# Finer weight pieces at the start of a hybrid decoder, and a final norm whose mean is summed on TensorE

## The chip, the cores and the metric

The kernel runs on one core of a Trainium2 chip. The metric is the device time of one launch in microseconds (us), lower is better. The engines of the core are TensorE (PE in the profile, with PEld for its weight loads), VectorE (DVE), ScalarE (ACT), GpSimd (POOL) and SyncE (SP, which here only issues transfers). Each engine takes its instructions from its own queue, and semaphores order them between engines.

## What is computed

One inference step of a decoder with two layers. Layer 0 mixes tokens with a short gated convolution, layer 1 with retention; behind each comes a SwiGLU feed-forward network, and at the end an RMS norm:

```python
def rmsnorm(x, g):
    y = x * rsqrt(mean(x * x, axis=-1) + 1e-6)
    return y * g

def short_conv_mixer(x, buf, w_in, w_conv, w_out):
    b, c, h = split(x @ w_in, 3)              # w_in: 1024 x 3072
    u = c * h
    full = concatenate([buf, u])
    y = sum(w_conv[j] * full[:, j:j+L] for j in range(3))
    return (b * y) @ w_out, full[:, -2:]

for i in range(2):
    x = x + mixer[i](rmsnorm(x, norm_mix[i]))  # short conv, then retention
    x = x + swiglu(rmsnorm(x, norm_ffn[i]))
y = rmsnorm(x, final_norm)
```

There are 512 prompt tokens and 8 x 4 sample tokens, 544 in all, with a model width of 1024 in fp32. The new convolution and retention states are outputs too.

## The kernel before

**Layout.** The activations stand transposed: x[kt], kt = 0 to 7, is a tile of 128 partitions (128 of the 1024 features) by 544 columns (the tokens). The columns are worked in two halves of 272 (HT): a matmul writes one half, `half(pt, hf)`. To keep fp32 accuracy with TensorE's faster type, every operand is split into a high and a low part, and each product is three matmuls: high weight by high activation, high weight by low activation, low weight by high activation (`project`, L187). A weight piece is loaded into a tile w; ScalarE copies the high part out of it (wh, L202) and VectorE subtracts to get the low part (wl, L203); `split` is the helper. The same is done for x by `split_x` (L221 on ScalarE, L222 on VectorE), which also multiplies in the norm's gain. The norm's own factor is taken out of the products: since it is one number for each token, the products start with x unscaled, and the factor is multiplied in later.

**The norm's factor.** `square_sum` squares a tile on ScalarE and adds it up on VectorE in sqacc. In the first stage and in several others it uses one buffer for the squares, sqlast (L238, added at L239; the last tile's at L234, L235). `rms_scale` then forms the mean over the features with matmuls that have sqacc as the stationary operand (L271, cb being the column of 1/1024), adds eps on VectorE (L244), takes the power −1/2 on GpSimd (L247, rN), and spreads the result over all partitions by a matmul against the identity (L251). The result is the row R.

**The start.** `start()` loads three weight pieces of 1024 columns (cvin 0 to 2, one for each of b, c and h) and the eight x tiles, and runs the products k tile by k tile as they come: for each of the eight k tiles, three pieces by three matmuls by two halves, 18 matmuls. So that k tile 0 can start early, each piece is loaded and split in column parts: first 128 columns (k tile 0), then k tiles 1 to 3 (384 columns), then 4 to 7 (512). The loads go out on SyncE's queue in the program's order, x[1], the second parts, x[2], x[3], the third parts, and so on; the splits are chained in the same order by `issue_after`, one behind the other, and behind the last one come the squares of x.

**The final norm.** `final` works on the last three output tiles (n = 5, 6, 7) of layer 1's feed-forward network, half by half. `products(hf)` makes the three products and adds them to x (L901), and squares each. `scale(hf)` is the norm's factor for one half: three sums of 128 columns or less (L919), eps (L920), pow (L921), then behind a `yield` the spread over the partitions (L251). `gained(hf)` multiplies x by the final gain into ya (x[0] to x[3]) and yb (x[4] to x[7]) at L911. `out(hf, y, w)` multiplies two of the tiles by the factor and stores them: for w = 0 ScalarE copies the factor to R (L932) and GpSimd does the multiplications (L934); for the others VectorE does (L936). The stores (L938) go out on ScalarE's queue for even w, on SyncE's for odd w. `idle(n, ins)` (L947) issues matmuls of ones whose result nobody reads.

**What sets the order.** The kernel is written in a tile framework: the program states what is done, a scheduler orders each engine's instructions, and `issue_after` binds an instruction behind another. Each engine then runs its instructions in the order given. In `final` the generators `products` and `scale` are advanced by hand (`next`, `drain`), which is how half 0's norm comes to stand among half 1's products.

## Time and profile before

| | |
|---|---|
| median of 3 runs | 1410.4 us (1409.67 to 1411.84) |
| the profiled execution | 1408.96 us, span 1407.2 us |
| granted TensorE clock, mean | 0.999 |
| TensorE busy | 1393.3 us (99%) |
| VectorE busy | 1133.3 us (81%) |
| ScalarE busy | 821.1 us (58%) |
| GpSimd busy | 216.2 us (15%) |
| moved by DMA | 233.82 MB, mean 166 GB/s |

How to read it: the span is from the first to the last instruction of the profiled execution, and the time of that execution holds a little more around it. Times in the timeline count from the span's start. A row of the timeline has the start, the length, the engine, the line, the operation, what is written and read, the shapes, and how many alike follow; in brackets stands how long the engine was idle before it and what ended that. The median of the runs and the profiled execution are different executions of the same program.

### The profile page before, as it was taken

How to read it: one execution, taken by the hardware profiler on the slowest of the kernel's cores; microseconds unless marked ns; L12 is line 12 of the kernel's file. 1: busy time of each engine (PE TensorE's matmuls, PEld its weight loads, DVE VectorE, ACT ScalarE, POOL GpSimd, SP SyncE). 2: the span in 40 equal slices, each digit the busy share in tenths (PEclk: the TensorE clock that was granted, in tenths of full speed). 3: DMA queues.
4: the chain of work that ended last, by engine and by line, in shares of the span. 5: the costliest groups of instructions: out<-in, count | busy, mean ns of one | idle time of the engine just before them, and what ended most of it. 6: DMA issues, size and time to landing. Idle time of an engine off the chain costs nothing.

```text
span 1407.2 us, 26615 instructions
## 1 busy us (share of the span) xinstructions
PE 1393.3 (99%) x10478; PEld 1320.4 (94%) x10478; DVE 1133.3 (81%) x1930; ACT 821.1 (58%) x1281; POOL 216.2 (15%) x248
## 2 busy tenths in 40 slices
PE   9999999999999999999999999999999999999997
PEld 8999999999999999999977877877899999999997
DVE  6987889898989878667867686585799898989884
ACT  6666567677667657667531413213387767677654
POOL 0111011222221214111000000010111212121212
PEclk9999999999999999999999999999999999999999
DMA  6466347768686745677567355375766777776742
GB/s 206 122 165 166 108 108 159 171 166 185 141 192 151 171 112 149 183 192 204 173 244 237 122 208 184 119 260 180 210 143 152 168 176 171 155 184 152 166 104 87
DMA packets 99246, 233.82 MB, mean 166 GB/s; under 512 B 9744, under 2 KB 33312, under 8 KB 98736
## 3 DMA queue, kind: packets, MB, share of 16 engines
q1 hardware_dynamic: 67696, 167.04, 38.0%
q0 software_dynamic: 28688, 56.61, 23.4%
q10 hardware_dynamic: 2736, 8.46, 1.6%
q8 instruction: 82, 1.34, 0.4%
q14 instruction: 44, 0.36, 0.1%
HBM read 191.97 MB, written 28.42 MB: 157 GB/s over the span
## 4 chain that ended last, share of the span: by engine, by line
PE 91%; DVE 4%; DMA 2%; ACT 1%; issue 1%; POOL 0%; SPq 0%; DVEq 0%; POOLq 0%; ACTq 0%
PE sm L385 43%; PE mm L385 16%; PE mm L187 13%; PE sm L187 5%; PE sm L1231 2%; PE sm L1229 2%; PE sm L1230 2%; PE sm L175 1%; PE sm L176 1%; PE sm L177 1%; PE sm L1452 1%; PE mm L1237 1%; DMA S<-in_rets_dram 1%; PE mm L1470 0%; DVE ol L203 0%
## 5 line engine op out<-in xcount | busy, mean ns | idle before, releaser
L385 PE MATMUL sm<-oh,wh 128*128 128x272 f32 x856 | 247.8, 289 | 0.5 <-DVE b L446 0.5
L385 PE MATMUL sm<-ol,wh 128*128 128x272 f32 x856 | 246.1, 288 | 0.0
L385 PE MATMUL sm<-oh,wl 128*128 128x272 f32 x856 | 246.1, 287 | 0.0
L202 ACT ACTIVATE h<-w 128x1024 fp32r<-128x1024 f32 (+3 forms) x170 | 136.6, 804 | 106.2 <-PE mm L385 92.9
L203 DVE TENSOR_TENSOR l<-w,h 128x1024 fp32r<-128x1024 f32 (+3 forms) x170 | 153.6, 905 | 28.1 <-ACT h L202 25.1
L314 ACT ACTIVATE wh<-w 128x1024 fp32r<-128x1024 f32 (+1 forms) x134 | 133.7, 998 | 56.9 <-PE sm L385 48.6
L385 PEld LDWEIGHTS sm<-oh,wh 128*128 128x128 f32 x856 | 161.3, 188 | 2.0 <-DVE b L446 0.9
L385 PEld LDWEIGHTS sm<-oh,wl 128*128 128x128 f32 x856 | 161.0, 188 | 0.0
L385 PEld LDWEIGHTS sm<-ol,wh 128*128 128x128 f32 x856 | 160.8, 188 | 0.1
L202 ACT ACTIVATE wh<-w 128x1024 fp32r<-128x1024 f32 (+3 forms) x76 | 67.7, 897 | 149.6 <-PE mm L187 92.9
L385 PE MATMUL sm<-parts,wh 128*128 128x272 f32 x736 | 142.5, 288 | 0.0
L317 POOL DMA_DIRECT2D wl<-in_ffgu_dram x87 | 81.7, 939 | 328.2 <-ACT wl L316 94.3
L385 PE MATMUL mm<-oh,h 128*128 128x272 f32 x396 | 115.5, 292 | 0.0
L385 PEld LDWEIGHTS sm<-parts,wh 128*128 128x128 f32 x736 | 115.5, 188 | 0.0
L385 PE MATMUL mm<-oh,l 128*128 128x272 f32 x396 | 113.5, 287 | 0.0
L385 PE MATMUL mm<-ol,h 128*128 128x272 f32 x396 | 113.3, 286 | 0.0
L315 DVE TENSOR_TENSOR wl<-w,wh 128x512 fp32r<-128x512 f32 (+1 forms) x134 | 87.3, 651 | 26.5 <-ACT wh L314 26.2
L385 PE MATMUL sm<-parts,wl 128*128 128x272 f32 x368 | 106.2, 289 | 0.3 <-DMA wl<-in_rtqk_dram 0.2
L316 ACT ACTIVATE wl<-wh 128x512 fp32r<-128x512 f32 (+1 forms) x173 | 102.9, 595 | 2.0
L203 DVE TENSOR_TENSOR wl<-w,wh 128x1024 fp32r<-128x1024 f32 (+3 forms) x76 | 79.5, 1055 | 12.6 <-ACT wh L202 12.2
L187 PE MATMUL mm<-parts,wh 128*128 128x272 f32 x488 | 83.1, 291 | 1.4 <-ACT wh L202 1.0
L385 PE MATMUL sm<-oh,h 128*128 128x272 f32 x284 | 82.3, 290 | 0.5 <-ACT g L444 0.3
(380 smaller groups left out, 3842.1 us busy)
## 6 DMA issues: line engine op xcount, KB each, us to landing
w<-in_ffgu_dram SPq DMA_DIRECT2D x66, 512.0 KB
wl<-in_ffgu_dram POOLq DMA_DIRECT2D x87, 256.0 KB, 5.2
S<-in_rets_dram SPq DMA_DIRECT2D x16, 1024.0 KB
out_rets_dram<-S SPq DMA_DIRECT2D x16, 1024.0 KB
w<-in_ffdn_dram SPq DMA_DIRECT2D x36, 384.0 KB
cb<-in_ffgu_dram SPq DMA_DIRECT2D x22, 512.0 KB
w<-in_cvin_dram SPq DMA_DIRECT2D x21, 512.0 KB
wl<-in_ffdn_dram POOLq DMA_DIRECT2D x48, 192.0 KB, 4.7
```

Source lines behind the costliest of these rows:

```text
L175: nc.tensor.matmul(out, lh, rh, start=start, stop=False, skip_group_check=True)
L187: last_product[0] = nc.tensor.matmul(half(pt, hf)[:, :HT], w[:, c], act[k][:, hf * HT : (hf + 1) * HT], start=(first and k == ks[0] and i ...
L202: h = nc.scalar.activation(dh, src, AF.Copy)
L203: last_low[0] = nc.vector.tensor_sub(dl, src, dh.bitcast(F32))
L314: nc.scalar.activation(wh, w, AF.Copy)
L315: last_mixed[0] = nc.vector.tensor_sub(wl[:, :n], w[:, :n], wh[:, :n].bitcast(F32))
L316: nc.scalar.activation(wl[:, n:], wh[:, n:].bitcast(F32), AF.Copy, scale=-1.0)
L317: nc.gpsimd.dma_start(wl[:, n:], src[:, 1, :] if len(src.shape) == 3 else src[:, n:], accum_op=ALU.add)
L385: last = nc.tensor.matmul(out, w[:, c], b, start=(first and j == 0 and i == 0), stop=(j == len(self.ks) - 1 and i == 2), skip_group_check= ...
L1229: nc.tensor.matmul(out, xh[kt][:, ts_], wh[:, cw], start=(kt == 0), stop=False)
L1230: nc.tensor.matmul(out, xh[kt][:, ts_], wl[:, cw], start=False, stop=False)
L1231: last = nc.tensor.matmul(out, xl[kt][:, ts_], wh[:, cw], start=False, stop=(kt == KT - 1))
```

## The change

The change has two parts.

In `start()` the three weight pieces come in five column parts, 128, 128, 256, 256 and 256 columns, where there were three of 128, 384 and 512. The second to fifth parts are loaded behind x[1], x[2], x[4] and x[6], where the second and third came behind x[1] and x[3]. Behind the first part there are thus 12 loads for 6, and 12 splits for 6.

In `final` half 1's products are issued in two parts of two and the remaining k tiles, so that other work can stand between them. Half 0's mean moves from behind product n = 5 of half 1 into the middle of n = 6, and half 0's spread from behind n = 7 into the middle of n = 7. In half 1 VectorE no longer adds the last square to sqacc: the means are summed over sqacc and sqlast by two groups of matmuls into the same place. The four idle matmuls go, the five remain. The outputs of half 0 are bound anew: w = 2 behind the last addition to x, half 1's eps behind the output of w = 2, w = 3 behind that eps.

```diff
     def square_sum(kt, pool, tag="sq", ..., add=None, apart=False):
...
             last_square[0] = nc.scalar.activation(sqlast[:, c], x[kt][:, c], AF.Square)
-            nc.vector.tensor_add(sqacc[:, c], sqacc[:, c], sqlast[:, c])
+            if not apart:
+                nc.vector.tensor_add(sqacc[:, c], sqacc[:, c], sqlast[:, c])
...
-            parts = [slice(0, P), slice(P, KP * P), slice(KP * P, KT * P)]
+            parts = [slice(0, P), slice(P, 2 * P), slice(2 * P, 4 * P), slice(4 * P, 6 * P), slice(6 * P, KT * P)]
...
                 nc.sync.dma_start(x[kt], a["xT"][kt])
-                if kt in (1, 3):
+                if kt in (1, 2, 4, 6):
                     for p in pieces:
-                        p[2](parts[1 + kt // 3])
-                        steps.append(lambda p=p, kt=kt: p[3](parts[1 + kt // 3]))
+                        p[2](parts[1 + kt // 2])
+                        steps.append(lambda p=p, kt=kt: p[3](parts[1 + kt // 2]))
...
-                project(pt, wh, wl, 0, ah, al, hfs=(hf,))
-                nc.vector.tensor_add(x[n][:, c], x[n][:, c], half(pt, hf)[:, :HT])
-                square_sum(n, tp, "gu", 4, c=c, add=nc.vector)
+                if hf:
+                    project(pt, wh, wl, 0, ah, al, last=False, hfs=(hf,), ks=range(2))
+                    yield
+                    project(pt, wh, wl, 0, ah, al, first=False, hfs=(hf,), ks=range(2, len(ah)))
+                else:
+                    project(pt, wh, wl, 0, ah, al, hfs=(hf,))
+                last_add[0] = nc.vector.tensor_add(x[n][:, c], x[n][:, c], half(pt, hf)[:, :HT])
+                square_sum(n, tp, "gu", 4, c=c, add=nc.vector, apart=hf == 1)
                 yield
...
-            for i, at in enumerate((0, P, HT - P)):
-                cols = slice(hf * HT + at, hf * HT + at + P)
-                last_sum[hf] = nc.tensor.matmul(mq[:, i : i + 1], sqacc[:, cols], mean_w[:, 0:1], start=True, stop=True)
-            nc.vector.tensor_scalar_add(rN[:, :3], mq, EPS)
+            for t in (sqacc, sqlast)[: hf + 1]:
+                for i, at in enumerate((0, P, HT - P)):
+                    cols = slice(hf * HT + at, hf * HT + at + P)
+                    last_sum[hf] = nc.tensor.matmul(
+                        mq[:, i : i + 1], t[:, cols], mean_w[:, 0:1],
+                        start=(t is sqacc and (i == 0 or not hf)), stop=(t is sqlast or not hf), skip_group_check=True,
+                    )
+            with tc.issue_after(last_out[0].ins) if hf else ExitStack():
+                last_eps[0] = nc.vector.tensor_scalar_add(rN[:, :3], mq, EPS)
...
         first, second = scale(0), products(1)
-        next(second)
+        for _ in range(3):
+            next(second)
         next(first)
         y0 = gained(0)
-        drain(second)
+        for _ in range(2):
+            next(second)
         drain(first)
         out(0, y0, 0)
         out(0, y0, 1)
-        idle(4, last_spread[0].ins)
+        drain(second)
+        with tc.issue_after(last_add[0].ins):
+            out(0, y0, 2)
         rest = scale(1)
         with tc.issue_after(last_spread[0].ins):
             next(rest)
         idle(5, last_sum[1].ins)
         y1 = gained(1)
-        out(0, y0, 2)
-        out(0, y0, 3)
+        with tc.issue_after(last_eps[0].ins):
+            out(0, y0, 3)
```

The scheduler makes of this the following. First ScalarE behind the first stage, where the squares of x and the splits of the next weights stand; x_74 to x_81 are x[0] to x[7], wh_354 and its like the high parts of the next 1024-column weights (other numbers in the changed program), b_111 and c_110 the copies of the first products. Before:

```order
L238 ACTIVATE sqlast<-x_76 128x544
L238 ACTIVATE sqlast<-x_77 128x544
L238 ACTIVATE sqlast<-x_78 128x544
L202 ACTIVATE wh_354<-w_353 128x1024
L238 ACTIVATE sqlast<-x_79 128x544
L593 ACTIVATE b_111<-mm_203 128x544
L593 ACTIVATE c_110<-mm_204 128x544
L202 ACTIVATE wh_418<-w_417 128x1024
L238 ACTIVATE sqlast<-x_80 128x544
```

After:

```order
L239 ACTIVATE sqlast<-x_76 128x544
L239 ACTIVATE sqlast<-x_77 128x544
L202 ACTIVATE wh_372<-w_371 128x1024
L239 ACTIVATE sqlast<-x_78 128x544
L594 ACTIVATE b_111<-mm_221 128x544
L594 ACTIVATE c_110<-mm_222 128x544
L202 ACTIVATE wh_436<-w_435 128x1024
L239 ACTIVATE sqlast<-x_79 128x544
L202 ACTIVATE wh_498<-w_497 128x1024
L239 ACTIVATE sqlast<-x_80 128x544
```

The first weight's split has moved ahead of the square of x[4], and the following squares stand behind more of other work.

Then ScalarE at the end of the program, with the semaphores that each instruction waits for (none are named where an engine waits for nothing new). Before:

```order
L238 ACTIVATE sq_16318<-x_80 128x272 [waits DVE_49,Activation_49]
L911 ACTIVATE yb_16364<-x_78,vec 128x272 [waits Activation_49]
L911 ACTIVATE yb_16364<-x_79,vec 128x272
L234 ACTIVATE sqlast<-x_81 128x272 [waits DVE_49]
L932 ACTIVATE R<-sm_16288 128x272 [waits PE_49]
L911 ACTIVATE yb_16364<-x_80,vec 128x272
L911 ACTIVATE yb_16364<-x_81,vec 128x272
L938 DMA out_yT_dram<-ya_16294 128x544 [waits Pool_49]
L938 DMA out_yT_dram<-yb_16295 128x544 [waits DVE_49,Activation_49]
L932 ACTIVATE R<-sm_16351 128x272 [waits PE_49]
```

After:

```order
L239 ACTIVATE sq_16336<-x_80 128x272 [waits DVE_49,Activation_49]
L943 ACTIVATE R<-sm_16313 128x272 [waits PE_49]
L917 ACTIVATE yb_16381<-x_78,vec 128x272 [waits Activation_49]
L917 ACTIVATE yb_16381<-x_79,vec 128x272
L949 DMA out_yT_dram<-ya_16319 128x544 [waits Pool_49]
L234 ACTIVATE sqlast<-x_81 128x272 [waits DVE_49]
L917 ACTIVATE yb_16381<-x_80,vec 128x272
L949 DMA out_yT_dram<-yb_16320 128x544 [waits DVE_49,Activation_49]
L917 ACTIVATE yb_16381<-x_81,vec 128x272
L943 ACTIVATE R<-sm_16365 128x272 [waits DVE_49,PE_49]
```

Half 0's copy of R and the store of ya, which waits for GpSimd, have moved ahead of the square of x[7].

Last, TensorE at the end of the program; sm_16288 (before) and sm_16313 (after) hold half 0's factor, sm_16351 and sm_16365 half 1's, sm_16321 and sm_16339 the product n = 7 of half 1. Before:

```order
L187 MATMUL sm_16321<-ol_11792,wh_16217 128x272
L187 MATMUL sm_16321<-oh_11791,wl_16218 128x272
L251 MATMUL sm_16288<-cb,rN 128x128 x2
L251 MATMUL sm_16288<-cb,rN 128x16
L947 MATMUL sm_16346<-ones 128x128 x4
L919 MATMUL sm_16351<-cb,sqacc 128x1 x3
L947 MATMUL sm_16357<-ones 128x128 x5
L251 MATMUL sm_16351<-cb,rN 128x128 x2
L251 MATMUL sm_16351<-cb,rN 128x16
```

After:

```order
L252 MATMUL sm_16313<-cb,rN 128x128 x2
L252 MATMUL sm_16313<-cb,rN 128x16
L187 MATMUL sm_16339<-parts,wh_16235 128x272 x2
L187 MATMUL sm_16339<-parts,wl_16236 128x272
L187 MATMUL sm_16339<-oh_11809,wh_16235 128x272
L187 MATMUL sm_16339<-ol_11810,wh_16235 128x272
L187 MATMUL sm_16339<-oh_11809,wl_16236 128x272
L926 MATMUL sm_16365<-cb,sqacc 128x1 x3
L926 MATMUL sm_16365<-cb,sqlast 128x1 x3
L958 MATMUL sm_16374<-ones 128x128 x5
L252 MATMUL sm_16365<-cb,rN 128x128 x2
L252 MATMUL sm_16365<-cb,rN 128x16
```

Half 0's spread now stands ahead of the last six matmuls of n = 7, the four idle matmuls are gone, and half 1's mean is two groups of three, the second on sqlast. The line numbers at the end of the changed program are 1 to 12 higher.

More of the change, by code (lines that the diff above doesn't have):

```diff
@@ L227, in hybrid_decode_kernel, with square_sum @@
     last_square = [None]
-    def square_sum(kt, pool, tag="sq", bufs=2, c=slice(0, T), first=0, last=KT - 1, add=None):
+    def square_sum(kt, pool, tag="sq", bufs=2, c=slice(0, T), first=0, last=KT - 1, add=None, apart=False):
         if kt == first:
@@ L935, in out @@
             else:
-                nc.vector.tensor_mul(yy, yy, sums[hf].unsqueeze(1).to_broadcast([P, 2, HT]))
+                last_out[0] = nc.vector.tensor_mul(yy, yy, sums[hf].unsqueeze(1).to_broadcast([P, 2, HT]))
             q = nc.sync if w % 2 else nc.scalar
             q.dma_start(o["yT"][hf][:, 2 * w : 2 * w + 2], yy)
-        last_sum, last_spread = {}, [None]
+        last_sum, last_spread, last_eps, last_out, last_add = {}, [None], [None], [None], [None]
         def idle(n, ins):
```

## Prediction

> **What bounds the kernel now.** I read the page first (span, busy shares, chain), then a table of stages, then the timelines of the start and of the end. From the page, the span, the busy times and the shares of the chain that ended last:
>
> ```profile
> span 1407.2 us, 26615 instructions
> PE 1393.3 (99%) x10478; PEld 1320.4 (94%) x10478; DVE 1133.3 (81%) x1930; ACT 821.1 (58%) x1281; POOL 216.2 (15%) x248
> PE 91%; DVE 4%; DMA 2%; ACT 1%; issue 1%; POOL 0%; SPq 0%; DVEq 0%; POOLq 0%; ACTq 0%
> ```
>
> The stages that the change touches, each with its length and then the busy time of PE, PEld, DVE, ACT and POOL, the granted clock, the DMA share and GB/s:
>
> ```profile
> 4.60:8.40 3.80, 2.79 (x18) 2.37 (x18) 1.75 (x6) 1.99 (x6) 0.00 (x0) 1.00 1.02 309
> 8.40:25.00 16.60, 16.40 (x126) 15.90 (x127) 11.29 (x18) 11.63 (x19) 0.00 (x0) 1.00 0.64 231
> 30.00:100.00 70.00, 70.00 (x559) 69.71 (x558) 63.76 (x108) 48.02 (x74) 11.89 (x13) 1.00 0.59 145
> 1388.00:1394.40 6.40, 6.22 (x51) 6.03 (x50) 3.09 (x9) 3.95 (x10) 1.01 (x1) 1.00 0.01 3
> 1394.40:1401.70 7.30, 4.29 (x36) 3.90 (x34) 4.88 (x9) 2.19 (x6) 3.77 (x5) 1.00 0.50 191
> ```
>
> TensorE is the bound: it is idle for 1407.2 − 1393.3 = 13.9 us in all. The change can win only in three places: about 1.0 us of idle ahead of 8.40, 0.2 up to 25, and the tail behind 1394, where a chain of short steps over all engines sets the end. Between 30 and 100 TensorE is never idle, and 70.00 / 559 gives 0.125 us for one matmul of 272 columns. The clock is 1.00 throughout, so it plays no part.
>
> **The start.** From the timeline: start, length, what ran, and in brackets the wait ahead of it.
>
> ```profile
> 4.90 0.49 ACT L202 ACTIVATE wh<-w 128x128 fp32r<-128x128 f32 x2
> 7.98 0.79 DVE L222 SCALAR_TENSOR_TENSOR parts<-x,vec,parts 128x544 fp32r<-128x544 f32 x1 [2.05 <-ACT parts L221]
> 8.41 0.93 PE L187 MATMUL mm<-parts,wh 128*128 128x272 f32 x4 [0.96 <-ACT wh L202]
> ...
> 18.17 0.66 ACT L238 ACTIVATE sqlast<-x 128x544 f32<-128x544 f32 x1 [0.67 <-DVE sqacc L239]
> 19.62 0.66 ACT L238 ACTIVATE sqlast<-x 128x544 f32<-128x544 f32 x1 [0.79 <-DVE sqacc L239]
> 23.54 1.06 ACT L202 ACTIVATE wh<-w 128x1024 fp32r<-128x1024 f32 x1 [1.80 <-PE mm L187]
> 24.50 0.64 ACT L238 ACTIVATE sqlast<-x 128x544 f32<-128x544 f32 x1
> 25.11 0.66 PE L187 MATMUL sm<-parts,wh 128*128 128x272 f32 x4
> ...
> 30.06 0.72 DVE L235 TENSOR_TENSOR sqacc<-sqacc,sqlast 128x544 f32<-128x544 f32 x1
> 31.06 1.17 PE L271 MATMUL mm<-cb,sqacc 128*128 128x1 f32 x10
> 32.51 1.31 POOL L247 TENSOR_TENSOR rN<-rN,expo 128x5 f32<-128x5 f32 x1 [31.67 <-DVE rN L244]
> 34.18 1.42 PE L251 MATMUL mm<-cb,rN 128*128 128x128 f32 x12
> ```
>
> *What goes.* At 8.41 TensorE had waited for a weight piece of 384 columns. A piece of 128 columns is split in 0.49 / 2 = 0.245 us, so wh would be there at about 8.15. But the second product needs the low part of x[1], which ends at 7.98 + 0.79 = 8.77 whatever the pieces. From there 16 of the tile's 18 matmuls, 16 × 0.125 = 2.0, end at 10.8; six more tiles of 18 × 0.125 = 2.25 each end at 24.3, provided that their operands are ready. The next product started at 25.11. The stage gains 0.8 at most.
>
> *What takes it back.* TensorE then meets the mean of squares at L271, and the squares lie on a chain of their own: ScalarE squares a tile into the one buffer sqlast, VectorE adds it, and only then comes the next square. A round took 19.62 − 18.17 = 1.45 us. In the program's order ScalarE now has the split wh of the next 1024-column weight, which waits for TensorE (1.80 us at 23.54), one square earlier: before x[4]'s square, where it stood behind it. That ScalarE takes work in order is seen at 24.50: that square stood behind the waiting split, while its turn by the rounds (22.5 at the latest, from 19.62 in steps of 1.45) was past. So the rounds behind the split are one more. The split moves with TensorE to 23.54 − 0.8 = 22.74; the last add ended at 30.06 + 0.72 = 30.78 and now ends at 30.78 − 0.8 + 1.45 = 31.43. TensorE gets to the mean after 48 matmuls where it was 44: 31.06 − 0.8 + 4 × 0.125 = 30.76. It waits there for about 0.7, and the mean starts at 31.47, 0.41 later, less the 0.50 of matmuls that are already done: −0.1. The pow on GpSimd ended 32.51 + 1.31 − 31.06 = 2.76 behind the mean's start: 34.23. TensorE, which has four matmuls fewer to put into this gap, reaches the spread (34.18) at 34.1 and waits until 34.27. I take **+0.1** for the start; the ends are −0.8 (the squares fit) and +0.5 (the squares' rounds also lose time to the three more splits of weights on both engines: 6 × 0.245 = 1.5 us on each, a third of it on the chain).
>
> **The middle.** Between 60 and 95 us the order of TensorE's products, and ScalarE's copies among them, comes out in another order, though the diff says nothing of it. The stage has no idle time to win (70.00 of 70.00), so it can only lose. The nearest wait in the trace of a product for such a sum is this one, of TensorE:
>
> ```profile
> 114.54 0.39 PE L385 MATMUL sm<-oh,wh 128*128 128x272 f32 x1 [0.46 <-DVE b L446]
> ```
>
> ScalarE's copy of a second partial sum now stands behind five more instructions. One or two such waits give 0 to 0.9; the order leaves TensorE other products to run meanwhile, so I take **+0.2**.
>
> **The tail.** The end in the order of the timeline, of all engines (ACTq and SPq are issues of stores):
>
> ```profile
> 1389.94 0.29 PE L187 MATMUL sm<-oh,wl 128*128 128x272 f32 x1
> 1390.41 0.80 PE L919 MATMUL sm<-cb,sqacc 128*128 128x1 f32 x6 [0.18 <-DVE sqacc L235]
> ...
> 1394.04 0.29 PE L187 MATMUL sm<-oh,wl 128*128 128x272 f32 x1
> 1394.17 0.74 PE L251 MATMUL sm<-cb,rN 128*128 128x128 f32 x6
> 1394.37 0.44 DVE L901 TENSOR_TENSOR x<-x,sm 128x272 f32<-128x272 f32 x1
> 1394.84 0.43 ACT L234 ACTIVATE sqlast<-x 128x272 f32<-128x272 f32 x1 [0.19 <-DVE x L901]
> 1395.17 0.38 ACT L932 ACTIVATE R<-sm 128x272 f32<-128x272 f32 x1
> 1395.30 0.44 DVE L235 TENSOR_TENSOR sqacc<-sqacc,sqlast 128x272 f32<-128x272 f32 x1 [0.49 <-ACT sqlast L234]
> 1395.63 1.48 POOL L934 TENSOR_TENSOR ya<-ya,R 128x272 f32<-128x272 f32 x2 [3.13 <-ACT R L932]
> 1395.66 0.71 DVE L936 TENSOR_TENSOR ya<-ya,sm 128x544 f32<-128x544 f32 x1
> 1395.80 0.83 PE L919 MATMUL sm<-cb,sqacc 128*128 128x1 f32 x6
> 1396.74 0.16 DVE L920 TENSOR_SCALAR rN<-sm 128x3 f32<-128x3 f32 x1 [0.36 <-PE sm L919]
> 1397.07 0.85 POOL L921 TENSOR_TENSOR rN<-rN,expo 128x3 f32<-128x3 f32 x1
> 1397.14 0.34 ACTq L938 DMA_DIRECT2D out_yT_dram<-ya  x1
> 1397.62 0.38 ACTq L938 DMA_DIRECT2D out_yT_dram<-yb  x1
> 1401.33 0.33 SPq L938 DMA_DIRECT2D out_yT_dram<-yb  x1
> ```
>
> The chain: last matmul, add of x[7], its square, VectorE's add into sqacc, the sums at 1395.80, eps, pow, spread, copy of R, outputs, last store at 1401.33.
>
> *Removed.* VectorE's add (1395.30 to 1395.80, with its way there, 0.5) leaves the chain: three matmuls read sqlast straight. Half 0's mean no longer stops TensorE: the last matmul of n=5 at 1389.94 would have been followed 0.125 later, the sums came at 1390.41, so a pause of some 0.37 goes, since in the middle of n=6 the add is long past. The four filling matmuls of 128 columns go too; they ran beside the chain and cost nothing.
>
> *Moved onto the path.* Half 0's spread (6 matmuls, 1394.17 to the fillers at 1394.75: 0.58) now runs ahead of the last product's second part. Last matmul: 1394.04 − 0.37 + 0.58 = 1394.25, done by 1394.56.
>
> *Made late.* Six matmuls stand behind the spread, so it starts at 1394.25 − 5 × 0.125 − 0.58 = 1393.05 (half 0's pow is just ready: the sums, six matmuls into n=6, start at about 1390.75, and from sums to pow's end half 1 took 1397.07 + 0.85 − 1395.80 = 2.1). It is done by 1393.8, and ScalarE copies R (0.38) by 1394.24; VectorE takes the output product of ya (0.71) from 1394.28 to 1395.0, and in its order that now stands ahead of the add of x[7]. The add goes from 1394.37 to 1394.95 and ends at 1395.39. On GpSimd, ya's two multiplications run from 1394.32 to 1395.80 (1.48). Their store is issued on ScalarE's queue, waits for GpSimd, and **in ScalarE's order now stands ahead of the last square**; before, it stood behind it. So the last square waits for GpSimd: the store at 1395.83, ScalarE free after one issue (1397.62 − 1397.14 = 0.48), the square at 1396.28 to 1396.71. The sums on sqlast start at 1396.75, where all sums began at 1395.80: +0.95. Behind them the steps are the same, but pow no longer stands behind GpSimd's multiplications (1395.63 + 1.48 = 1397.11, against an eps that ended at 1396.90): 0.1 back. Queued behind the waiting store are also two of yb's gains and its store, which come before the copy of R in good time. I take **+0.9**. Ends: if the store does not hold ScalarE, the square starts at 1395.42, the sums at 1395.89, and the end moves by 0.0 (or −0.35 if VectorE's product came behind the add); if the issue holds it twice as long, +1.3.
>
> **Sum.** +0.1 + 0.2 + 0.9 = +1.2. The profiled execution took 1408.96 (span 1407.2 and 1.76 around it), so it would take 1410.2. The median of the runs shown is 1410.4, 1.4 above the profiled one; on it, **1411.6**. That is +0.09%, while what a measurement of this kernel can tell from no change is about 0.2%, 2.8 us: *same*.
>
> **The rivals.**
>
> *A, the gain arrives.* The squares' rounds fit in beside the splits, since two of the weights' pieces are shorter, and the store does not hold the square. Then −0.8 at the start, 0 to +0.2 in the middle, −0.35 to 0.0 in the tail: about −0.8, 1409.6. For it speaks that both waits at the start are seen and go. Against it: both orders that take it back stand in the program, and ScalarE is in order at 24.50. Chance 0.24, a tenth of it beyond 2.8 us if a wait that I don't see goes too.
>
> *B, slower: the loads of small pieces come late.* Twelve loads stand among x[2] to x[7] for six, rows shorter. What decides is x[7]'s landing, because the squares start behind its split.
>
> ```profile
> 13.48 2.81 ACT L221 ACTIVATE parts<-x,vec 128x544 fp32r<-128x544 f32 x4
> DMA packets 569, 0.47 MB, mean 233 GB/s; under 512 B 104, under 2 KB 460, under 8 KB 569
> DMA packets 415, 0.80 MB, mean 398 GB/s; under 512 B 46, under 2 KB 46, under 8 KB 415
> ```
>
> Four splits of x from 13.48 in 2.81 put x[7]'s at 15.6. The second and third rows are 3 to 5 us, where pieces of 128 columns (64 KB) move, and 11 to 13 us, where longer ones do: 233 and 398 GB/s. Behind x[1] lie 3 × 448 KB of weights and 6 × 272 KB of x, 3.05 MB; at 233 GB/s for all of it x[7] would land 13.1 us behind x[1] (its split starts at 7.2), at 20.3. From x[7]'s split to the end of x[3]'s square it takes 4.7 us (15.6 to 19.62 + 0.66 = 20.3), and the split of wh frees at 22.74, so a landing after 18.0 pushes the squares, and the mean, one for one: 20.3 costs 2.3 on top of 1411.6, **1413.9**. It is slower by over 0.2% if x[7] lands after 19.6. Against it: half of the weights still come in 256-column pieces, and 398 GB/s was reached with those of 512. Chance 0.12, three quarters of it beyond 2.8 us.
>
> On this the Trainium skill (DMA: Bandwidth & Descriptors, section Bandwidth) speaks against the change: it tells to batch moves to 1 MiB or more, with 138 GB/s for one of 64 KB and 341 for 1 MB, on GpSimd's queue. By its small figure for the twelve pieces, x[7] would land at about 21.4 and the time be about 1415, an estimate from that page. The trace's 233 GB/s with 64 KB pieces in flight says that several transfers of this queue overlap, so I give it no more than B's chance.
>
> **How the numbers follow.** Forecast (the orders on ScalarE decide) 0.60, A 0.24, B 0.12, anything else 0.04. The forecast's own bounds are −0.8 + 0 + 0.0 to +0.5 + 0.9 + 1.3, rarely together; 1410.3 to 1413.0. The range reaches down to A's lower end, 1410.4 − 1.1 and half a microsecond for the scatter of three runs (1409.67 to 1411.84), 1408.8, and up to 1413.6, which takes in B for landings before 20.0. Faster by over 0.2%: a tenth of A and part of the rest, 0.03. Slower: three quarters of B and a little of the rest, 0.11. Same: 0.86.
>
> **What would show it.** In the changed profile: the pause at 8.4 shorter and the first product behind the k tiles at 24.3 (else the start's gain is wrong); one square ahead of the wh split that waits on TensorE fewer, and TensorE waiting for sqacc ahead of the mean near 31 (else the +0.1 is −0.8); between 60 and 95 us waits of at most 0.5; the last square starting behind the store's issue, at GpSimd's end and not at the add's end, and the sums on sqlast about 2.4 us behind the last matmul's start (1396.75 − 1394.25 = 2.5; before, 1395.80 − 1394.04 = 1.76). If the square starts as soon as x[7]'s add ends, the tail term is wrong and A is right there. If x[7]'s split starts after 18, B is.

## The result, and the profile after

The changed kernel takes 1413.17 us (median of 14 runs, 1411.08 to 1415.37), the kernel before 1410.43 in the runs beside it (14 runs, 1407.38 to 1411.84). The ratio is 1.0026, with a 95% interval of 1.0019 to 1.0033: slower by about a quarter of a per cent (the medians lie 2.7 us apart; the ratio stands for 3.7 us, its interval for 2.7 to 4.7). The prediction had 1411.6 in a range of 1408.8 to 1413.6 and gave 0.86 to *no difference*; the time lies in the range, but the kernel is slower, which had 0.11. That it lies in the range is luck: the forecast's own upper bound was 1413.0, and the range reached up to 1413.6 only to take in rival B, which did not come.

The profiled execution has a span of 1410.1 for 1407.2: 2.9 us to explain. The line numbers of the changed kernel are 1 to 11 higher from `square_sum` on in the rows shown (L251 is L252 there, L938 is L949), and those of runs that add lines are higher again. First the start, from the timelines of the changed kernel:

```profile
16.49 0.75 ACT L221 ACTIVATE parts<-x,vec 128x544 fp32r<-128x544 f32 x1
23.95 0.66 PE L187 MATMUL sm<-parts,wh 128*128 128x272 f32 x4
30.34 0.72 DVE L236 TENSOR_TENSOR sqacc<-sqacc,sqlast 128x544 f32<-128x544 f32 x1 [0.72 <-ACT sqlast L234]
31.12 1.28 PE L272 MATMUL mm<-cb,sqacc 128*128 128x1 f32 x10 [0.60 <-DVE sqacc L236]
32.52 1.22 DVE L203 TENSOR_TENSOR wl<-w,wh 128x1024 fp32r<-128x1024 f32 x1
32.68 2.09 POOL L248 TENSOR_TENSOR rN<-rN,expo 128x5 f32<-128x5 f32 x1 [31.84 <-DVE rN L245]
34.82 1.38 PE L252 MATMUL mm<-cb,rN 128*128 128x128 f32 x10 [0.81 <-POOL rN L248]
```

The k tiles end 1.16 earlier (23.95 for 25.11), and TensorE then waits 0.60 for the last square's sum ahead of the mean. Both were predicted, the gain at 0.8 at most. But the power on GpSimd takes 2.09 us for 1.31, TensorE waits another 0.81 for it, and the first spread comes at 34.82 for 34.18: **+0.64**.

The middle, from the timelines of the changed kernel (SPq: a weight load is issued; DVE: the instruction that waits for it; PE: the waits in this stretch):

```profile
96.51 2.56 SPq L333 DMA_DIRECT2D w<-in_cvin_dram  x2
102.98 0.69 DVE L337 TENSOR_TENSOR w<-w,w 128x512 f32<-128x512 f32 x1 [3.32 <-DMA w<-in_cvin_dram]
111.46 0.52 PE L386 MATMUL mm<-parts,h 128*128 128x272 f32 x2 [0.93 <-ACT b L445]
116.09 0.39 PE L386 MATMUL sm<-oh,wh 128*128 128x272 f32 x1 [0.46 <-DVE b L447]
```

and the same load in the kernel before:

```profile
95.09 3.29 SPq L332 DMA_DIRECT2D w<-in_cvin_dram  x2
101.43 0.69 DVE L336 TENSOR_TENSOR w<-w,w 128x512 f32<-128x512 f32 x1 [2.46 <-DMA w<-in_cvin_dram]
```

The wait at 116.09 is the one that stood at 114.54 before, 1.55 later. The wait of 0.93 is new: **+0.91** in this stretch. Counted from the first spread, the load is issued at 61.69 for 60.91 before. From here to the final norm nothing more is lost between these two executions: the last matmul of n = 5 is at 1391.37 for 1389.94, +1.43.

The tail, all engines, from the timeline of the changed kernel:

```profile
1392.25 0.72 PE L926 MATMUL sm<-cb,sqacc 128*128 128x1 f32 x6
1395.72 0.28 PE L187 MATMUL sm<-oh,wl 128*128 128x272 f32 x1
1395.68 1.49 POOL L945 TENSOR_TENSOR ya<-ya,R 128x272 f32<-128x272 f32 x2 [1.41 <-ACT R L943]
1396.27 0.43 DVE L907 TENSOR_TENSOR x<-x,sm 128x272 f32<-128x272 f32 x1
1397.19 0.34 ACTq L949 DMA_DIRECT2D out_yT_dram<-ya  x1
1397.58 0.43 ACT L234 ACTIVATE sqlast<-x 128x272 f32<-128x272 f32 x1 [1.16 <-DVE yb L947]
1398.07 0.83 PE L926 MATMUL sm<-cb,sqlast 128*128 128x1 f32 x6 [1.50 <-ACT sqlast L234]
1399.24 0.85 POOL L932 TENSOR_TENSOR rN<-rN,expo 128x3 f32<-128x3 f32 x1 [2.08 <-DVE rN L931]
1400.40 1.30 PE L252 MATMUL sm<-cb,rN 128*128 128x128 f32 x6
1404.21 0.33 SPq L949 DMA_DIRECT2D out_yT_dram<-yb  x1
```

The last addition to x ends at 1396.70, but its square starts at 1397.58, behind the store's issue at 1397.19, which waited for GpSimd until 1397.17. (The bracket puts the wait down to VectorE's product of yb; the run `e4_store` below shows that it is the store.) The sums on sqlast stand at 1398.07 for 1395.80, 0.84 more than the offset of 1.43. Behind them comes what the prediction had not priced: the spread takes 1.30 us for 0.84 and starts 0.31 behind the power's end, where it was 0.05. The table of stretches (length, busy times of PE, PEld, DVE, ACT, POOL, granted clock, DMA share, GB/s) shows why, in the changed kernel:

```profile
1396.00:1398.00 2.00, 0.57 (x7) 0.48 (x5) 1.33 (x3) 0.84 (x4) 1.16 (x2) 1.00 0.36 139
1398.00:1400.00 2.00, 1.94 (x15) 1.94 (x16) 0.79 (x2) 0.84 (x3) 0.76 (x1) 0.87 0.73 279
1400.00:1402.00 2.00, 1.70 (x9) 1.59 (x8) 0.00 (x0) 0.27 (x1) 0.09 (x1) 0.50 0.35 139
```

and in the kernel before, over the same two last stretches:

```profile
1398.00:1400.00 2.00, 0.81 (x6) 0.71 (x6) 0.88 (x3) 0.40 (x1) 0.68 (x1) 1.00 1.01 384
1400.00:1402.00 2.00, 0.00 (x0) 0.00 (x0) 1.26 (x3) 0.00 (x0) 0.80 (x2) 1.00 0.60 227
```

TensorE's granted clock falls to half: 0.87 over the stretch from 1398 to 1400 means at about 1399.5, and from there on it is 0.50. TensorE had stood still from 1396.57 (the end of the sums on sqacc) to 1398.07. The last store is at 1404.21 for 1401.33, +2.88, so the tail costs **+1.45**. The three losses, 0.64 + 0.91 + 1.45, less 0.12 given back between the middle and the tail, are the 2.88 between these two executions.

### The profile page after: what moved, and what is told of

The parts are those of the page before. It is cut to its first block, busy times and chain, and to the rows that moved or that the text cites. A ratio compares the mean times of both kernels' runs of the same rounds, so it can differ in the third digit from the quotient of the medians.

```text
span 1410.1 us, 26630 instructions
## 1 busy us (share of the span) xinstructions
PE 1393.8 (99%) x10476; PEld 1321.7 (94%) x10476; DVE 1133.2 (80%) x1935; ACT 821.1 (58%) x1287; POOL 216.9 (15%) x248
## 4 chain that ended last, share of the span: by engine, by line
PE 90%; DVE 5%; DMA 2%; ACT 1%; issue 1%; POOL 0%; DVEq 0%; ACTq 0%; SPq 0%; POOLq 0%
PE sm L386 42%; PE mm L386 16%; PE mm L187 13%; PE sm L187 4%; PE sm L1244 2%; PE sm L1246 2%; PE sm L1245 2%; PE sm L175 1%; PE sm L176 1%; PE sm L177 1%; PE sm L1467 1%; DVE ol L203 1%; PE mm L1252 1%; DMA S<-in_rets_dram 1%; PE mm L1485 0%
## 5 line engine op out<-in xcount | busy, mean ns | idle before, releaser
L203 DVE TENSOR_TENSOR l<-w,h 128x1024 fp32r<-128x1024 f32 (+3 forms) x170 | 153.8, 905 | 25.4 <-ACT h L202 22.5
L203 DVE TENSOR_TENSOR wl<-w,wh 128x1024 fp32r<-128x1024 f32 (+3 forms) x82 | 80.1, 990 | 11.8 <-ACT wh L202 11.4
```

The lines of the kernel that those rows point to most:

```text
L203: last_low[0] = nc.vector.tensor_sub(dl, src, dh.bitcast(F32))
```

## The experiments

The theory (T in the expectations) was that these are three separate losses. Each run is compared with the kernel before on the same chip, 5 rounds each. An interval of these ratios is some ±0.1%, 1.4 us, wide; where a step is smaller than that, the profile carries the verdict and the time does not. To compare tails, I take the time from half 0's sums to the last store: 1404.21 − 1392.25 = 11.96 in the change. Before, the sums stood elsewhere; from the last matmul of n = 5 it was 11.39, and in the change the sums come 1392.25 − 1391.37 = 0.88 behind that matmul, so the like of it before is 10.51.

**The two parts alone.** `e1_start` has the first part of the change, `e2_final` the second:

```diff
 e1: parts = five pieces, loads behind x[1], x[2], x[4], x[6]; final() as before
 e2: final() and square_sum() as changed; start() as before
```

> Only the first part of the change: weight pieces of k tiles in five column parts, the final norm as before. Theory T (three separate losses, of which the first two belong to the start): the mean of squares waits for the squares' rounds, half-power on GpSimd takes 2.09 us rather than 1.31 beside VectorE's split, so the first spread is 0.64 us later; VectorE frees a weight buffer 1.4 us later near 96 us, its load lands later, and TensorE waits 0.93 near 111 us. Together +1.5 us over the kernel before, the profile's wait of 0.9 for a copy near 111 present, the tail as before. Rival S (the start gains what it was seen to save, 1.16 us at the end of the k tiles, and the loss lies in the tail): -1.2 to 0 us.

> Only the second part of the change: the final norm as changed, the start in three column parts as before. Theory T: the tail alone loses 1.45 us: +0.25 up to the last product, +0.6 because the last square stands behind the store that waits for GpSimd, and 0.6 to 0.7 because TensorE's clock falls after its pause. So +1.4 us over the kernel before, a pause of about 1.5 us ahead of the sums on sqlast and a granted clock under 0.8 behind them. Rival S: the tail alone carries the whole difference, +2.9 us. Rival N: the tail is neutral and all of it comes from start and middle, 0 us.

Measured: e1 1.0020 (1.0012 to 1.0029), e2 1.0018 (1.0009 to 1.0027). Either part alone is slower, so neither rival S holds. Waits of TensorE in e1 (the first two rows, timeline), and the tail in e2 (the last three):

```profile
34.88 1.38 PE L251 MATMUL mm<-cb,rN 128*128 128x128 f32 x10 [0.81 <-POOL rN L247]
112.17 0.52 PE L385 MATMUL mm<-parts,h 128*128 128x272 f32 x2 [1.50 <-ACT b L444]
```

```profile
1392.83 0.72 PE L926 MATMUL sm<-cb,sqacc 128*128 128x1 f32 x6
1398.65 0.83 PE L926 MATMUL sm<-cb,sqlast 128*128 128x1 f32 x6 [1.50 <-ACT sqlast L234]
1404.70 0.33 SPq L949 DMA_DIRECT2D out_yT_dram<-yb  x1
```

e1 has both waits of the start and the one of the middle, there even 1.50, and its tail is that of before (11.36 from the last matmul of n = 5, at 1393.10, to the last store at 1404.46; before 11.39). e2 has no wait near 111 us and the tail of the change: 11.87. The sum of the two, +0.38%, is more than the whole change's +0.26%, but within the intervals.

Neither has the size that theory T gave. e1's profile is 3.1 us over before (span 1410.3) and its time 2.8 (1.7 to 4.1), where T had 1.5. The profiles of the other runs show why. The start as before stands in five of them (before, e2, e7, e10, e11). There the first spread comes at 33.09 to 34.38, in the mean at 33.70, and the marker that stands at 114.54 before comes at 112.90 to 114.56, in the mean at 113.80. The changed start, with the order behind it untouched, stands in four (the change, e1, e3, e4): the spread at 34.56 to 34.88, mean 34.75, the marker at 115.88 to 116.80, mean 116.19. So the profile of the kernel before shows one of its late starts. In the mean the first spread loses 1.05 for 0.64, and the stretch behind it 1.35 for 0.91. With the tail's 1.45 that makes 3.8 us, near the ratio's 3.7. e2's profile is 3.4 over before (span 1410.6), and its tail is 1.36 of it. Most of the rest lies far from the change: TensorE waits 2.67 for loads of the retention states, where it waited 0.92 before, and behind the longest of these waits (2.48, up to 993.33) its granted clock is 0.50 between 995 and 997.

**The tail: the clock and the store.** `e3_fill` puts idle matmuls into TensorE's pause, `e4_store` takes the store off ScalarE's queue:

```diff
 e3, in scale(1), behind the sums on sqacc:
+                if hf and t is sqacc:
+                    idle(5, last_sum[1].ins)
 e4, in out():
-            q = nc.sync if w % 2 else nc.scalar
+            q = nc.sync if w % 2 or (hf, w) == (0, 0) else nc.scalar
```

> The whole change, with five more idle matmuls on TensorE between the sums on sqacc and the sums on sqlast (1.4 us of work in a pause of 1.5 us). Theory T: the clock stays at 1.00 to the end and the last spread takes 0.84 us for 1.30, so 0.6 to 0.7 us faster than the whole change; the square still stands behind the store. Rival C (the clock falls because the load is light near the end, not because of that pause, or the spread is long for another reason): no gain, or up to 0.1 us slower because the sums stand behind the idle matmuls.

> The whole change, with the first store of half 0 (ya, the one that waits for GpSimd) issued from SyncE's queue, so that ScalarE's last square no longer stands behind it. Theory T: the last square starts when the last addition to x ends, 0.85 us earlier, TensorE's pause shrinks from 1.5 to 0.65 us; 0.85 us faster than the whole change, and 1.5 us faster if the shorter pause also keeps the clock. Rival V (the square waits for VectorE's product of yb, which the trace of waits names, and not for the store): no gain.

From the timeline of e3:

```profile
1392.18 0.72 PE L926 MATMUL sm<-cb,sqacc 128*128 128x1 f32 x6
1398.00 0.83 PE L926 MATMUL sm<-cb,sqlast 128*128 128x1 f32 x6 [0.28 <-ACT sqlast L234]
1400.09 0.84 PE L252 MATMUL sm<-cb,rN 128*128 128x128 f32 x6
1403.44 0.33 SPq L951 DMA_DIRECT2D out_yT_dram<-yb  x1
```

and of e4:

```profile
1392.22 0.72 PE L926 MATMUL sm<-cb,sqacc 128*128 128x1 f32 x6
1396.24 0.43 DVE L907 TENSOR_TENSOR x<-x,sm 128x272 f32<-128x272 f32 x1
1396.70 0.43 ACT L234 ACTIVATE sqlast<-x 128x272 f32<-128x272 f32 x1 [0.32 <-DVE x L907]
1397.19 0.83 PE L926 MATMUL sm<-cb,sqlast 128*128 128x1 f32 x6 [0.65 <-ACT sqlast L234]
1399.53 1.30 PE L252 MATMUL sm<-cb,rN 128*128 128x128 f32 x6
1403.34 0.33 SPq L949 DMA_DIRECT2D out_yT_dram<-yb  x1
```

In e3 the square is as late as ever (sums at 5.82 behind half 0's sums, in the change too), but the clock stays and the spread takes 0.84: tail 11.26, 0.70 less. In e4 the square starts as the addition ends, and the sums come 0.85 earlier (4.97); VectorE's yb, named in the bracket, was not its cause. The clock falls even behind a pause of 0.65: tail 11.12. The times, 1.0025 (1.0015 to 1.0035) and 1.0026 (1.0016 to 1.0037), cannot tell steps of 0.7 and 0.8 from nothing. The granted clock of the other executions can: half the clock for the last 10.6 us, as in the change's profile, takes 0.004 off a program's mean. That mean is 0.9963 over the 14 executions of the change and 0.9983 over the 9 of e3, where the kernel before has 0.998. In e4 it lies between 0.992 and 0.999, so behind the shorter pause the clock seems to fall in some executions only.

`e7_tail` has both cures on the start as before, so the whole tail can be seen in the time:

```diff
 e7: e2, with the store on SyncE's queue and idle(4, last_sum[1].ins) between the sums
```

> The start as before; the final norm as changed, but with half 0's first store on SyncE's queue and four idle matmuls between the sums on sqacc and those on sqlast. Theory T: the square starts 0.85 earlier and the clock stays 1.00 to the end, 1.5 us faster than the changed final norm alone, so the kernel before -0.1 us: no difference. Rival: the clock falls all the same, or the sums stand behind the idle matmuls: +0.6 us over before.

Measured 1.0000 (0.9991 to 1.0008), where e2 had 1.0018. The changed norm's loss is gone, with a tail of 10.49 in its profile (1389.59 to 1400.08), as before (10.51). So these two causes are the tail's loss, and by the profile all of it.

**The start.** `e5_squares` gives the squares a second buffer; `e6_pow` keeps VectorE still beside the first power:

```diff
 e5, squares of start() (shortened):
-            sq = pool.tile(...) if pool else sqlast
+            sq = pool.tile(...) if pool else (R if kt % 2 == 0 else sqlast)
 e6, in rsqrt(), for the first call (shortened; the next weight's low part is bound behind it):
         nc.gpsimd.tensor_tensor(out, out, expo[: out.shape[0], :n], op=ALU.pow)
+        if n == 5 and not held_once:
+            held_once.append(nc.vector.tensor_copy(fe[:, 0, 0:1], out[:, 0:1]))
```

> The whole change, with the squares of the first stage written by turns into two buffers (sqlast and the still unused R), so that a square no longer waits for the addition of the one before. The scheduler then puts short subtractions of 272 columns behind eps on VectorE, where the whole change has a weight's split of 1024 columns. Theory T: the mean no longer waits for sqacc (0.6 us), and the power on GpSimd, which ended 1.03 us behind the end of VectorE's instruction beside it both before (32.79 to 33.82) and after (33.74 to 34.77), takes 1.3 us or less for 2.09. So 1.4 us earlier at the first spread; and if TensorE's wait of 0.9 near 111 us comes from VectorE being late since the start, that goes too: 1.4 to 2.3 us faster than the whole change. Rival M (the middle's wait belongs to the order there and not to the start): 1.4 and the wait stays. Rival Z (the start is bound by the loads): no gain.

> The whole change, with VectorE kept idle beside the first power: a copy of one column of its result stands behind eps on VectorE and waits for it, and the weight's split of 1024 columns comes behind that copy. Theory L (the power waits until VectorE's instruction with two operands in memory has ended): it takes 0.9 to 1.1 us for 2.09, TensorE's wait of 0.81 for it goes, the first spread stands 0.8 earlier. VectorE loses about 1.1 us, so its wait near 111 us may grow by as much: by the time between 0.8 faster and 0.3 slower. Rival: the power takes 2.09 whatever VectorE does (its first use, or its five columns); the spread stays and VectorE's delay makes the kernel 0 to 1.1 slower.

From the timelines of e5:

```profile
29.16 0.43 DVE L529 TENSOR_TENSOR f<-f 128x272 f32<-128x272 f32 x1
29.32 1.30 POOL L248 TENSOR_TENSOR rN<-rN,expo 128x5 f32<-128x5 f32 x1 [28.48 <-DVE rN L245]
32.73 1.42 PE L252 MATMUL mm<-cb,rN 128*128 128x128 f32 x12
109.46 0.52 PE L386 MATMUL mm<-parts,h 128*128 128x272 f32 x2 [0.75 <-ACT b L445]
```

and of e6:

```profile
32.41 1.17 POOL L250 TENSOR_TENSOR rN<-rN,expo 128x5 f32<-128x5 f32 x1 [31.56 <-DVE rN L247]
33.63 1.52 PE L256 MATMUL mm<-cb,rN 128*128 128x128 f32 x12
111.23 0.52 PE L390 MATMUL mm<-parts,h 128*128 128x272 f32 x2 [1.14 <-ACT b L449]
```

In the kernel before, VectorE ran this beside the power (32.51 to 33.82):

```profile
32.35 0.44 DVE L529 TENSOR_TENSOR f<-f 128x272 f32<-128x272 f32 x1
```

In e5 the mean no longer waits, a subtraction of 0.43 stands beside the power, and the power ends 1.03 behind that subtraction's end (29.59 to 30.62). The spread comes at 32.73, 2.09 earlier than in the change, more than the 1.4 expected, since the scheduler also put the mean earlier. In e6, with nothing beside it, the power takes 1.17, the spread comes 2.78 behind the mean's start (33.63 − 30.85; in the change 34.82 − 31.12 = 3.70), and TensorE's wait for it is gone. So the power's length is set by what VectorE runs. Near 111 us TensorE still waits, 0.75 in e5 and 1.14 in e6, as rival M of e5 had it. e5 keeps its gain over the change up to the marker, which stands at 114.09 for 116.09. e6 does not: its spread is 1.19 earlier, and the product near 111 starts only 0.23 earlier.

The times do not confirm the gains. e5 has 1.0014 (1.0005 to 1.0024), an interval that overlaps with the change's. Its profile is even longer than the change's (span 1411.4), with a wait of 2.46 for a load of the states and the clock at 0.50 between 995 and 996 behind it, as in e2. e6 has 1.0040 (1.0026 to 1.0054, six executions), 5.6 us over before, where its profile has 3.9 (span 1411.1) and the expectation allowed 0.3 over the change. In its profile the clock falls at 1398.0, earlier than in the change, and its tail is 13.14 for 11.96; why the kernel is this slow is open.

**The middle.** `e9_relief` leaves out one multiplication of VectorE ahead of the split that frees the weight's buffer:

```diff
                     r = sqlast.unsqueeze(1).to_broadcast([P, 2, T])
-                    nc.vector.tensor_mul(pair[1], pair[1], r)
+                    if f != 4:
+                        nc.vector.tensor_mul(pair[1], pair[1], r)
```

> The whole change, with one multiplication of VectorE left out: the scaling of the convolution's c for the second pair of tiles (128x1088, 1.28 us, at 94.56 in the trace of the change), so that the instruction behind it, the weight's split that frees a buffer, comes 1.28 us earlier, and with it the load's issue at 96.51. The order of all engines is otherwise the same. Part of the convolution is thus not scaled. Theory Q (TensorE's wait near 111 is the lateness of VectorE's split, passed on by the load, VectorE's next products and ScalarE's copy): the load is issued near 95.2, VectorE's product that waits for it starts near 101.7, and TensorE's wait of 0.93 is under 0.1; 0.9 us faster than the whole change. Rival B (the load lands when the other transfers of that stretch leave it room): it lands near 102.9 all the same and the wait stays at 0.8 to 1.0.

From the timelines of e9:

```profile
34.80 1.38 PE L252 MATMUL mm<-cb,rN 128*128 128x128 f32 x10 [0.83 <-POOL rN L248]
95.34 3.80 SPq L333 DMA_DIRECT2D w<-in_cvin_dram  x2
101.78 0.69 DVE L337 TENSOR_TENSOR w<-w,w 128x512 f32<-128x512 f32 x1 [2.04 <-DMA w<-in_cvin_dram]
114.88 0.39 PE L386 MATMUL sm<-oh,wh 128*128 128x272 f32 x1 [0.39 <-DVE b L447]
```

The load is issued 1.17 earlier, lands as much earlier, and the wait near 111 is gone: from the first spread to the marker at 114.88 it takes 80.08, where the change took 116.09 − 34.82 = 81.27 and the kernel before 114.54 − 34.18 = 80.36. So theory Q holds, and the load's own time (6.4 us from its issue to VectorE's start in e9, 6.5 in the change) did not grow. It shows how the lateness is passed on; what made VectorE late by then, no run shows. Span 1409.1 for 1410.1; the time, 1.0023 (1.0013 to 1.0032), cannot tell this.

**All three at once, and a better tail.** `e8_both` joins e5 and e7's tail; `e10_add` is e7 with the addition to x ahead of ya's product on VectorE, `e11_two` that with two idle matmuls for four:

```diff
 e8: e5, with the store on SyncE's queue and idle(4, last_sum[1].ins) between the sums
 e10: e7, with
         out(0, y0, 0)
-        out(0, y0, 1)
         drain(second)
         with tc.issue_after(last_add[0].ins):
-            out(0, y0, 2)
+            out(0, y0, 1)
+        last_out[0] = last_add[0]
...
         with tc.issue_after(last_eps[0].ins):
+            out(0, y0, 2)
             out(0, y0, 3)
 e11: e10, with
-                    idle(4, last_sum[1].ins)
+                    idle(2, last_sum[1].ins)
```

> The start with five pieces and two buffers for the squares, and the final norm with the store on SyncE's queue and four idle matmuls: all three causes taken away. Theory T: at the first spread 0.75 earlier than the kernel before, 0 to 0.9 lost near 111 us, tail -0.1: between 0.9 faster and 0.1 slower than the kernel before, where the whole change is 3 to 3.7 slower. Rival (a cause is missing): it stays 1 us or more slower than before.

> The tail once more, on the start as before: the store on SyncE's queue and four idle matmuls between the two groups of sums, and besides the last addition to x stands ahead of the output product of ya (0.72 us) on VectorE, which it stood behind. Theory T: the addition starts as the last product ends, 0.2 to 0.3 us earlier, and the sums, the power, the spread and the last store follow it: from half 0's sums to the last store 10.2 us for 10.5. In the time that is -0.3 us against the kernel before, which the measurement cannot tell from no change. Rival: eps, now behind ya's product on VectorE, or the power behind GpSimd's multiplications takes it back: 10.5.

> The tail with the addition ahead of ya's product, as in the run before, but with two idle matmuls in place of four between the two groups of sums. There the last square ended 0.46 ahead of the sums on sqlast, and four idle matmuls stood between. Theory T: the sums on sqlast start as the square ends, 0.4 earlier; the pause that is left is under 0.6 us and the clock stays 1.00; from half 0's sums to the last store 10.1 us for 10.5. In the time 0.3 to 0.4 us under the kernel before, less than the measurement tells. Rival: the shorter cover lets the clock fall, and the spread takes 1.30 for 0.84: 10.8.

e8: 1.0007 (0.9999 to 1.0016), with a span of 1407.2, that of before. Its first spread is at 33.27, 0.91 earlier than in the profile before, a wait of 0.43 is left near 109 us, and at the marker near 114 it is still 0.73 ahead (113.81 for 114.54). Both lie inside the ranges of the start as before (33.09 to 34.38, 112.90 to 114.56), so what is shown is that the start's loss is gone, and no gain. The 0.73 goes to waits further on, which differ between executions of one order too: in all these profiles TensorE waits between 0.9 and 2.7 for loads of the states (1.8 in e8, 0.9 before). e10: 1.0005 (0.9995 to 1.0014); the addition is 0.21 earlier against half 0's sums, but the four idle matmuls still stood ahead of the sums on sqlast when the square was done, and the tail stayed at 10.50. e11, from its timeline:

```profile
1391.17 0.72 PE L926 MATMUL sm<-cb,sqacc 128*128 128x1 f32 x6
1395.94 0.83 PE L926 MATMUL sm<-cb,sqlast 128*128 128x1 f32 x6
1398.02 0.84 PE L252 MATMUL sm<-cb,rN 128*128 128x128 f32 x6
1401.38 0.33 SPq L951 DMA_DIRECT2D out_yT_dram<-yb  x1
```

Its tail is 10.21, the shortest of all, with the clock at 1.00; 0.9993 (0.9983 to 1.0003) says that it is at most 0.03% slower than the kernel before. A gain of 0.3 us is below what the time tells.

## Why the prediction was wrong, step by step

- **The squares: right. The start's gain: right in direction, wrong in its bound.** 0.8 at most was forecast at the end of the k tiles, 1.16 came. The bound stood on the low part of x[1], which "ends at 7.98 + 0.79 = 8.77 whatever the pieces". In the change it ended at 7.60, since x[1]'s split on ScalarE started at 6.03 for 7.20: at 5.80 to 6.16 in all eight profiles with the small pieces, at 6.26 to 7.87 in the five with the large ones. On the squares, TensorE was to wait about 0.7 for the squares, it waited 0.60; the mean came at 31.12, 31.47 was forecast. e5 shows the rounds of squares to be the cause of that wait.
- **The step that failed at the start** is "The pow on GpSimd ended … = 2.76 behind the mean's start". I carried that gap over as a constant. It holds the power's 1.31, and that depends on VectorE: the change put a weight's split of 1.22 us beside it for a subtraction of 0.44. The gap became 3.65 (31.12 to 34.77), 0.89 longer, of which the power is 0.78. The mean was 0.35 earlier than forecast, and the term came to +0.64 for +0.1, outside its upper bound of +0.5; in the mean of the profiles it is 1.05.
- **The middle: "One or two such waits give 0 to 0.9", of which I took +0.2.** It was 0.91, just past the upper bound (1.35 in the mean of the profiles), and not where I looked: not between 60 and 95 us for a copied sum, but near 111, passed on from VectorE's split through a load to a copy (e9). "The order leaves TensorE other products to run meanwhile" failed: TensorE's products waited all the same. That VectorE, 63.76 of 70.00 busy before, had no room to catch up is argued, not shown.
- **The tail up to the sums: right.** The spread ahead of the last product cost 0.25 (0.21 forecast); the store held the square, and the sums came 0.84 late with that (0.95 forecast). e4 shows the cause.
- **The step that failed in the tail** is "The four filling matmuls … ran beside the chain and cost nothing". Their removal was priced at nothing. With them gone and the square late, TensorE stood still for 1.50, the clock fell, and the steps behind cost 0.7 more; with idle matmuls in that pause the clock stays at 1.00 and the 0.7 is gone (e3). "The clock is 1.00 throughout, so it plays no part" was read from the kernel before, in which the fillers stood. With this the tail came to +1.45, outside its upper end of +1.3.
- **Rival A** (the gain arrives) fell at both places. **Rival B** (late loads) fell too: x[7]'s split started at 16.49, far ahead of the 18.0 from which it would decide; the small pieces did not hold the start. The estimate of 1415 from the Trainium skill's figure for small transfers fell with it.
- **The sum** was +1.2 against +2.9. All three terms were too small, by 0.54, 0.71 and 0.55. The chances followed from the sum: with 1411.6 as the likeliest, slower by 2.8 us was left to rival B alone, and the failed terms had no part in it.

## What to carry to other kernels

An instruction's duration from the trace is that of its neighbours too: before carrying it over, look at what the other engine runs beside it after the change. Work that computes nothing may still cover a pause, so ask what TensorE's clock does when it goes. A store put on a computing engine's queue is an instruction of that queue: here the last square stood behind one until the store's data was there, 0.85 us (e4). And one profile of each kernel is a pair of executions: here the start of the kernel before varied by 1.3 us between profiles, more than the term that was to be explained.

## What the runs showed of the hardware

- The first power on GpSimd (128x5) ended 1.03 or 1.04 us behind the end of the VectorE instruction that was running when it started, in all twelve profiles that have one: 32.79 to 33.82 before (L529, 0.44 long), 33.74 to 34.77 after (L203, 1.22 long), 29.59 to 30.62 in e5 (0.43 long). With VectorE idle it took 1.17 (e6). The Trainium skill (SBUF — State Buffer, section "SBUF: two separate sides") says that VectorE with two operands in SBUF and a GpSimd instruction that reads SBUF share ports exclusively: the one that starts first has them for its whole instruction, and the other blocks. The traces agree as far as the power stands behind VectorE's instruction. They do not show the reverse: in the kernel before, VectorE ran subtractions of tiles at 32.71 and 33.06, while the power lasted until 33.82.
- The granted clock fell to 0.50 after TensorE had waited 1.50 us (the change, e2) and 0.65 us (e4) for the last square, and stayed at 1.00 with a wait of 0.28 (e3) and with none (e7, e11). The length of a wait alone does not decide: the clock fell behind one of 2.48 near 993 us (e2), and stayed at 1.00 behind one of 1.83 there (e8) and one of 1.50 near 112 us (e1). The Trainium skill (TensorE: Matmul & The Clock Gate, section "What's actually happening") has the clock go down after an idle window of about 3.4 us; here pauses of 0.65 to 2.48 us were enough in some places. What decides between them, no run shows.
